# 45 small matmuls with an unread result, between the first modulation and the first projection of a hybrid backbone step

## The chip, the cores and the metric

The kernel runs as one program on one core of a Trainium2 chip. The metric is the device time of one execution in microseconds (us). Below, PE is TensorE (matmuls), PEld its loading of stationary operands, DVE is VectorE, ACT is ScalarE, POOL is GpSimd and SP the engine that issues most DMAs. PSUM is the memory that PE writes its results to: eight banks, each 512 fp32 columns on 128 partitions.

## The reference

One inference step of four layers over 128 context tokens and 512 latent tokens, 1024 features wide. Each layer modulates its input with a shift, a scale and a gate that come from a conditioning vector, runs a token mixer (differential attention, bidirectional retention, short convolution, differential attention), and ends in a residual layer norm:

```python
def ada_modulation(cvec, w_mod, b_mod):
    m = jax.nn.silu(cvec) @ w_mod + b_mod
    shift, scale, gate = jnp.split(m[:, None, :], 3, axis=-1)
    return shift, scale, gate
...
    for i in range(DEPTH):
        sh_p, sc_p, g_p = ada_modulation(c_ctx[None], w_mod[i], b_mod[i])
        sh_s, sc_s, g_s = ada_modulation(c, w_mod[i], b_mod[i])
        hp = xp * (1 + sc_p) + sh_p
        hs = xs * (1 + sc_s) + sh_s
...
            q, k, v, z = diff_project(hp, w_in_a[j])
...
        xp = layer_norm(ALPHA * xp + g_p * out_p, ln_g[i], ln_b[i])
        xs = layer_norm(ALPHA * xs + g_s * out_s, ln_g[i], ln_b[i])
```

## The kernel before

All tokens lie transposed in SBUF (`xT`: features on partitions, 640 token columns). Matrix products are made in three matmuls of rounded halves (`mm3`: high by high, low by high, high by low), so each weight block `raw` that a DMA brings in is first split into `wh` on ACT and `wl` on DVE (`convert`), and each modulated input into `hH` and `hL`.

The order of the work on the engines is fixed when the program is built: a planner walks over streams of small items with a cost for each operation, takes the item that it thinks starts soonest, and writes its instructions down. Every engine then runs its own list in order and waits on counters of the other engines (semaphores, one per engine: a wait is for a count). Which waits an instruction needs is worked out when it is written down, from the tiles and the ranges of them that it and earlier instructions read and write. All of PSUM is one tile, `ps`.

The first stage matters here. The shift and scale of layer 0 are computed in four parts of 256 features. For each part `pair_mm` does 32 plain fp32 matmuls, in two blocks of 16: the conditioning vector, padded to 32 columns (`cpad`), is the stationary operand, 128 columns of `w_mod` are the moving one, and the four results of one step `k` go to the four strips of 32 partitions of bank `m0`. `pair_vectors` then copies the 128 x 128 result to SBUF on ACT (`mdt`), transposes it on PE into columns 128 to 256 of the same bank (`tr`, line 477), adds the bias on DVE in two instructions (`mod`) and makes the scale and shift vectors `Av` and `Bv` on DVE. With them `first_h` computes the modulated input, hH on ACT and its unrounded copy `FA` on ACT or DVE; `first_lo` makes hL. The first projection of layer 0, matmuls of hH or hL with wh or wl (line 469), follows on PE. The first item that PE has after the transposition of part 0 is this projection.

A plain fp32 matmul (both operands fp32 and not rounded) is one row in the program's order and two MATMUL records in the trace, one behind the other; a transposition is one record.

Of the kernel before, what the change touches and what calls it, by code (L numbers as in the profile page):

```python
# [234 lines left out]
def kernel(ctx: ExitStack, tc: tile.TileContext, io: dict):  # L235
    nc = tc.nc
# [3 lines left out]
    def sb(name, shape, dt=F32):  # L240
        return big.tile(shape, dt, name=name)
# [14 lines left out]
    ident = sb("ident", [128, 128])  # L256
    rope0, KD, rope3 = [big.tile([128, 2 * TS], dt, name=n, tag="rope") for n, dt in (("rope0", F32), ("KD", F32R), ("rope3", F32))]
    cpad = sb("cpad", [128, KC, 32])
# [82 lines left out]
    def bank(key):  # L341
        b, n = S.held[key]
        return PS[:, b] if n == 1 else PS[:, b:b + n]

    def done(key):
        b, n = S.held.pop(key)
        S.free += range(b, b + n)
# [11 lines left out]
    def isap(x):  # L359
        return x is not None and not isinstance(x, (int, float))  # L360

    def do(eng, dur, outs, ins, emit, port=False):
        if S.rec is None:
            emit()
        else:
            S.rec.append((eng, dur, outs, [a for a in ins if isap(a)], port))
# [5 lines left out]
    def n_of(ap):  # L372
        n = 1
        for _, c in list(ap.ap)[1:]:
            n *= c
        return n

    def act(out, in_, func=ACTF.Copy, **k):
        extra = [k.get("scale"), k.get("bias")]
        outs = [out] + ([k["accum_out"]] if "accum_out" in k else [])  # L380
        d = n_of(out) / 1.2 + (51 if in_.tensor.name == PS.tensor.name else 94) + 93 * (sum(map(isap, extra)) + len(outs) - 1)
        do("ACT", d, outs, [in_] + extra, lambda: nc.scalar.activation(out=out, in_=in_, func=func, **k))  # L382

    def vtt(out, a, b, op):
        do("DVE", n_of(out) / 0.96 + 70, [out], [a, b], lambda: nc.vector.tensor_tensor(out=out, in0=a, in1=b, op=op), both(a, b))  # L385
# [23 lines left out]
    def vts(out, a, s1, s2=None, op0=ALU.mult, op1=None):  # L409
        k = {} if s2 is None else {"op1": op1}  # L410
        do("DVE", n_of(out) / 1.4 + 70 + 50 * (isap(s1) + isap(s2)), [out], [a, s1, s2],
           lambda: nc.vector.tensor_scalar(out=out, in0=a, scalar1=s1, scalar2=s2, op0=op0, **k), both(a, out))  # L412
# [13 lines left out]
    def vcopy(out, a):  # L426
        do("DVE", n_of(out) / 0.96 + 70, [out], [a], lambda: nc.vector.tensor_copy(out=out, in_=a))
# [33 lines left out]
    def mm(out, lhsT, rhs, start, stop):  # L461
        n = list(rhs.ap)[-1][1] if len(list(rhs.ap)) == 2 else n_of(rhs)
        m = n_of(lhsT)
        if lhsT.dtype == F32:
            d = n * {1: 112.0, 256: 1.88, 384: 2.5}.get(n, 1.69) if m > 32 else n / 2.4
        else:
            d = max(n / 2.4 + 13.5, 110.0 if m > 32 else 0.0)
        do("PE", d, [out], [lhsT, rhs],
           lambda: nc.tensor.matmul(out, lhsT=lhsT, rhs=rhs, start=start, stop=stop, skip_group_check=True))  # L469
# [6 lines left out]
    def tr(out, a):  # L476
        do("PE", 116.0, [out], [a], lambda: nc.tensor.transpose(out, a, ident))  # L477
# [984 lines left out]
    def pair_mm(p, ks):  # L1462
        MD = bank("m0") if ks[0] else pj("m0")
        for k in ks:
            for j in range(4):
                mm(MD[32 * j:32 * j + 32, 0:128], cpad[:, k, :], wt0[p % 2][k // 4][:, k % 4, 128 * j:128 * j + 128], k == 0, k == 7)

    def pair_vectors(p):
        MD = bank("m0")
        mt = mdt[:, 128 * (p % 2):128 * (p % 2) + 128]  # L1470
        act(mt, MD[:, 0:128])
        tr(MD[:, 128:256], mt)
        for g in range(2):
            c = slice(8 * g + 2 * p, 8 * g + 2 * p + 2)
            vtt(
                mods[0][:, c, :],
                MD[:, 128 + 64 * g:192 + 64 * g].rearrange("p (j r) -> p j r", r=32)[:, :, 0:2],
                bmod[:, 0, c].unsqueeze(2).to_broadcast([128, 2, 2]),
                ALU.add,
            )  # L1480
        done("m0")
        c = slice(2 * p, 2 * p + 2)
        vts(Av[0][:, c, :], mods[0][:, 8 + 2 * p:10 + 2 * p, :], 1.0, op0=ALU.add)
        vcopy(Bv[0][:, c, :], mods[0][:, c, :])
# [31 lines left out]
    for p in range(4):  # L1516
        if p:
            ld0.append(Item(lambda p=p: load_pair(p), need=[("m0", p - 2) if p > 1 else ("start",)], give=[("ld", p)]))
        for k in range(0, 8, 4):
            st0.append(Item(lambda p=p, k=k: pair_mm(p, range(k, k + 4)), need=[("ld", p)] if p else (),  # L1520
                            give=[("m0", p)] if k else ()))
        st0.append(Item(lambda p=p: pair_vectors(p)))
        for m in (2 * p, 2 * p + 1):
            for hf in range(2):
                need = [("lnh", -1, hf, m - 4)] if m > 3 else []
                st0.append(Item(lambda m=m, hf=hf: first_h(m, hf), need=need, give=[("t", -1, hf, m)]))
                lo0.append(Item(lambda m=m, hf=hf: first_lo(m, hf), need=[("t", -1, hf, m)], give=[("lnh", -1, hf, m)]))
            x0.append(Item(lambda m=m: first_x(m), need=[("t", -1, 1, m)], give=[("lnx", -1, 0), ("lnx", -1, 1)] if m == 7 else ()))
# [353 lines left out]
```

## Time and profile before

| | |
|---|---|
| time, median of three runs | 1816.77 us (1816.58 to 1816.88) |
| the profiled execution | 1815.59 us, of which span 1813.8 us |
| mean granted clock of PE over the span | 0.986 of full speed |
| PE busy | 1756.9 us, 97% of the span |
| PEld, DVE, ACT, POOL busy | 1652.1, 1123.9, 724.0, 128.8 us |
| DMA | 186.80 MB, mean 103 GB/s |

The span goes from the first to the last instruction on the profiled core; 1.79 us of the profiled execution lie around it. Busy shares are averages over stages with different limits, so the first 24 us are read by themselves below. The clock column (PEclk) gives the share of full speed that was granted to PE: 1.00 is 2.4 GHz, 0.50 is 1.2 GHz, a value between is a stretch with both.

### The profile page before, as it was taken

The page shows a single profiled execution, that of the slowest core. Times are in us where ns is not written, and L with a number is a line of the kernel's source. Part 1 is how long each engine was busy: PE and PEld are TensorE (multiplying, and loading weights), DVE is VectorE, ACT ScalarE, POOL GpSimd, SP SyncE. Part 2 cuts the span into 40 slices and gives each one's busy share as a digit, 9 for nine tenths or more (in the row PEclk, how much of TensorE's full clock was granted, in tenths as well). Part 3 has the DMA queues.
Part 4 walks back from the last instruction along what each step waited for, and adds up shares of the span by engine and source line. Part 5 has one row for each costly group of instructions (what it writes and reads, how often), then busy time and mean ns, then how long its engine had stood idle before and what let it go on. Part 6 is the DMA issues. An engine that isn't in the chain of part 4 may idle for free.

```text
span 1813.8 us, 31795 instructions
## 1 busy us (share of the span) xinstructions
PE 1756.9 (97%) x12756; PEld 1652.1 (91%) x12756; DVE 1123.9 (62%) x2673; ACT 724.0 (40%) x1546; POOL 128.8 (7%) x133
## 2 busy tenths in 40 slices
PE   7999999999999999999999989999999999999996
PEld 6999999999889889888888889999999999999995
DVE  3877777888726335245434674344368767778877
ACT  4555555544424323223223333222225545555441
POOL 1001000002300000000000013000003210000101
PEclk8999999999999999999999999999999999999998
DMA  9533333226312233321321351233345222222201
GB/s 348 165 114 114 114 114 96 74 73 166 107 70 97 82 115 117 105 93 57 117 93 47 116 161 50 100 129 122 105 124 150 68 67 80 81 75 63 73 16 59
DMA packets 76309, 186.80 MB, mean 103 GB/s; under 512 B 9600, under 2 KB 20992, under 8 KB 75136
## 3 DMA queue, kind: packets, MB, share of 16 engines
q1 hardware_dynamic: 74432, 178.47, 29.8%
q0 software_dynamic: 1728, 6.29, 1.9%
q8 instruction: 100, 1.64, 0.4%
q14 instruction: 49, 0.40, 0.1%
HBM read 159.04 MB, written 8.91 MB: 93 GB/s over the span
## 4 chain that ended last, share of the span: by engine, by line
PE 83%; DVE 10%; ACT 4%; issue 2%; DMA 1%; SPq 0%; POOL 0%; ACTq 0%; DVEq 0%; POOLq 0%
PE ps L469 80%; PE ps L477 4%; DVE xT L416 1%; DVE sm L416 1%; DVE wl L385 1%; ACT wh L382 1%; ACT FA L382 1%; ACT F L382 1%; DVE F L385 1%; DVE FA L439 1%; DVE xT L385 1%; DVE F L416 0%; DVE sm L430 0%; DVE FA L412 0%; DVE sm L385 0%
## 5 line engine op out<-in xcount | busy, mean ns | idle before, releaser
L469 PE MATMUL ps<-hH,wh 128*128 128x256 f32 (+1 forms) x1184 | 374.5, 316 | 4.7 <-ACT wh L382 3.1
L469 PE MATMUL ps<-hH,wl 128*128 128x256 f32 (+1 forms) x1184 | 366.6, 310 | 1.4 <-DVE wl L385 1.4
L469 PE MATMUL ps<-hL,wh 128*128 128x256 f32 (+1 forms) x1184 | 366.6, 310 | 0.0
L385 DVE TENSOR_TENSOR wl<-raw,wh 128x1024 fp32r<-128x1024 f32 (+2 forms) x177 | 208.1, 1178 | 246.4 <-ACT wh L382 245.5
L469 PE MATMUL ps<-wh,hH 128*128 128x256 f32 (+1 forms) x960 | 310.9, 324 | 1.2 <-DVE F L416 1.0
L382 ACT ACTIVATE wh<-raw 128x1024 fp32r<-128x1024 f32 (+2 forms) x198 | 198.1, 1003 | 285.1 <-PE ps L469 208.4
L469 PE MATMUL ps<-wl,hH 128*128 128x256 f32 (+1 forms) x960 | 305.9, 319 | 0.0
L469 PE MATMUL ps<-wh,hL 128*128 128x256 f32 (+1 forms) x960 | 305.8, 319 | 0.0
L469 PEld LDWEIGHTS ps<-hH,wh 128*128 128x128 f32 x1184 | 225.1, 190 | 11.1 <-issue 4.3
L469 PEld LDWEIGHTS ps<-hH,wl 128*128 128x128 f32 x1184 | 225.2, 190 | 2.1 <-DVE wl L385 1.9
L469 PEld LDWEIGHTS ps<-hL,wh 128*128 128x128 f32 x1184 | 224.9, 190 | 0.3 <-DVE hL L385 0.3
L469 PE MATMUL ps<-yh,wh 128*128 128x384 f32 (+1 forms) x640 | 203.5, 318 | 5.0 <-ACT yh L382 4.3
L469 PE MATMUL ps<-yl,wh 128*128 128x384 f32 (+1 forms) x640 | 199.4, 312 | 0.0
L469 PEld LDWEIGHTS ps<-wh,hH 128*128 128x128 f32 x960 | 182.8, 190 | 17.9 <-ACT FA L382 1.8
L469 PE MATMUL ps<-yh,wl 128*128 128x384 f32 (+1 forms) x640 | 198.9, 311 | 0.0
L469 PEld LDWEIGHTS ps<-wl,hH 128*128 128x128 f32 x960 | 182.7, 190 | 12.7
L469 PEld LDWEIGHTS ps<-wh,hL 128*128 128x128 f32 x960 | 182.8, 190 | 11.8
L382 ACT ACTIVATE FA<-FA,sm 128x640 f32<-128x640 f32 x144 | 112.0, 778 | 164.7 <-DVE sm L439 164.7
L416 DVE SCALAR_TENSOR_TENSOR xT<-ps,mod,xT 128x128 f32<-128x128 f32 (+2 forms) x312 | 121.6, 435 | 77.6 <-PE ps L469 77.3
L382 ACT ACTIVATE F<-ps 128x128 f32<-128x128 f32 (+2 forms) x336 | 97.5, 318 | 154.3 <-PE ps L469 151.7
L469 PE MATMUL ps<-RA 128*128 128x320 f32 (+2 forms) x696 | 129.5, 320 | 1.8 <-DVE F L416 1.1
L469 PEld LDWEIGHTS ps<-yh,wh 128*128 128x128 f32 x640 | 122.5, 191 | 8.5 <-ACT yh L382 4.7
(155 smaller groups left out, 2583.2 us busy)
## 6 DMA issues: line engine op xcount, KB each, us to landing
mraw<-in_w_mod SPq DMA_DIRECT2D x160, 256.0 KB, 4.6
raw<-in_wqk_a SPq DMA_DIRECT2D x32, 512.0 KB, 3.5
raw<-in_wvz_a SPq DMA_DIRECT2D x32, 512.0 KB, 4.0
raw<-in_wvg_b SPq DMA_DIRECT2D x32, 512.0 KB, 3.3
raw<-in_win_c SPq DMA_DIRECT2D x32, 512.0 KB, 3.2
RA<-RA SPq DMA_DIRECT2D x32, 320.0 KB, 4.0
raw<-in_wqk_b SPq DMA_DIRECT2D x16, 512.0 KB, 3.2
raw<-in_wout_b SPq DMA_DIRECT2D x16, 512.0 KB, 3.2
```

Source lines behind the costliest of these rows:

```text
L382: do("ACT", d, outs, [in_] + extra, lambda: nc.scalar.activation(out=out, in_=in_, func=func, **k))
L385: do("DVE", n_of(out) / 0.96 + 70, [out], [a, b], lambda: nc.vector.tensor_tensor(out=out, in0=a, in1=b, op=op), both(a, b))
L416: lambda: nc.vector.scalar_tensor_tensor(out=out, in0=a, scalar=s, in1=b, op0=op0, op1=op1), both(a, b))
L439: do("DVE", n_of(out) / 0.96 + 68, [out, mx], [a], lambda: nc.vector.tensor_tensor_reduce(out=out, in0=a, in1=z, scale=-0.125, scalar=3.0e ...
L469: lambda: nc.tensor.matmul(out, lhsT=lhsT, rhs=rhs, start=start, stop=stop, skip_group_check=True))
L477: do("PE", 116.0, [out], [a], lambda: nc.tensor.transpose(out, a, ident))
```

## The change

`stay_awake` writes fp32 matmuls of one `cpad` block with the identity matrix, 32 output partitions by 128 columns, into columns 256 to 384 of bank `m0`, partitions 0 to 31, which nothing reads. For part 0 alone, five of them stand ahead of the transposition and forty behind it.

```diff
+    def stay_awake(MD, n):
+
+        for i in range(n):
+            do("PE", 0.0, [MD[0:32, 256:384]], [cpad[:, i % 8], ident],
+               lambda i=i: nc.tensor.matmul(MD[0:32, 256:384], lhsT=cpad[:, i % 8, :], rhs=ident, start=True, stop=True, skip_group_check=True))
+
     def pair_vectors(p):
         MD = bank("m0")
         mt = mdt[:, 128 * (p % 2):128 * (p % 2) + 128]
         act(mt, MD[:, 0:128])
+        if p == 0:
+            stay_awake(MD, 5)
         tr(MD[:, 128:256], mt)
+        if p == 0:
+            stay_awake(MD, 40)
         for g in range(2):
             c = slice(8 * g + 2 * p, 8 * g + 2 * p + 2)
             vtt(
```

The planner counts them as 0 ns, so that the rest of every engine's list stands as before. On PE, from the second block of part 0 (the `cpad` rows) to the first projection (`ps<-hH,wh`), with the engines whose counters a row waits for in brackets (DMAHW are DMA queues):

```order
 L469 MATMUL ps<-F_92,cpad 32x128 [waits DMAHW2_49]
 L469 MATMUL ps<-F_92,cpad 32x128 x15
-L477 MATMUL ps<-ident,mdt 128x128 [waits DMAHW3_49,Activation_49]
+L1472 MATMUL ps<-ident,cpad 32x128 [waits DMAHW3_49,Activation_49]
+L1472 MATMUL ps<-ident,cpad 32x128 x4
+L477 MATMUL ps<-ident,mdt 128x128
+L1472 MATMUL ps<-ident,cpad 32x128 x40
 L469 MATMUL ps<-hH,wh_73 128x256 [waits Activation_49]
 L469 MATMUL ps<-hH,wl_77 128x256 [waits DVE_49]
```

The 45 new rows stand around the transposition, and the wait for ACT (the copy of the bank to `mdt`) that the transposition had now stands at the first of them. On DVE, from the padding of `cpad` to the vectors `Av` and `Bv`; the first `mod` row is the bias add of part 0:

```order
 L412 TENSOR_SCALAR cvec<-cvec 128x16 [waits DVE_49]
 L427 COPY cpad<-cvec 128x8x2 [waits DVE_49]
-L385 TENSOR_TENSOR mod_107<-ps,bmod 128x4 [waits DMAHW4_49,PE_49]
+L385 TENSOR_TENSOR mod_107<-ps,bmod 128x4 [waits DMAHW4_49,PE_49,Activation_49]
 L385 TENSOR_TENSOR mod_107<-ps,bmod 128x4
 L412 TENSOR_SCALAR Av_109<-mod_107 128x4 [waits DVE_49]
```

The bias add waits for PE in both; only its wait for ACT is new in these rows. The count of PE that it waits for is not printed in them; in the built programs it is 33 before (16 and 16 for the two blocks of `pair_mm`, 1 for the transposition) and 78 now, and PE now adds its 46 (45 new matmuls and the transposition) in one step, at the last of the forty.

## Rows read from the trace of the kernel before

**Rows 1.** The page: busy time by engine, and the granted clock in 40 slices.
```profile
PE 1756.9 (97%) x12756; PEld 1652.1 (91%) x12756; DVE 1123.9 (62%) x2673; ACT 724.0 (40%) x1546; POOL 128.8 (7%) x133
...
PEclk8999999999999999999999999999999999999998
```

**Rows 2.** The chain that ended last, 9 to 22 us: start, us, what.
```profile
9.10 1.55 PE ps L469 x32
...
10.67 0.29 ACT mdt L382
10.96 0.04 issue
11.00 0.34 PE ps L477
11.34 0.02 issue
11.37 0.24 DVE mod L385 x2
...
11.91 0.49 ACT hH L382
...
18.05 1.24 DVE wl L385
19.28 0.04 issue
19.32 2.86 PE ps L469 x26
```

**Rows 3.** Stretches of the first 40 us: busy us by engine, PEclk, DMA share, GB/s.
```profile
11.40:13.40 2.00, 0.00 (x0) 0.00 (x0) 0.79 (x5) 1.49 (x4) 0.15 (x1) 1.00 1.03 418
13.40:14.10 0.70, 0.00 (x0) 0.00 (x0) 0.00 (x0) 0.70 (x2) 0.58 (x1) 0.51 1.04 421
14.10:19.30 5.20, 3.29 (x7) 1.86 (x7) 4.33 (x7) 4.86 (x9) 1.53 (x2) 0.50 1.00 415
19.30:23.60 4.30, 4.28 (x40) 3.57 (x41) 1.57 (x2) 0.00 (x0) 0.00 (x0) 0.50 1.07 414
23.60:24.30 0.70, 0.70 (x6) 0.45 (x5) 0.00 (x0) 0.00 (x0) 0.00 (x0) 0.96 0.99 398
24.30:40.00 15.70, 15.70 (x193) 14.64 (x196) 8.42 (x24) 9.14 (x20) 2.91 (x3) 1.00 1.03 399
```

**Rows 4.** PE in order of time: start, busy us, instruction, idle before.
```profile
11.00 0.33 PE L477 MATMUL ps<-ident,mdt 128*128 128x128 f32 x1 [0.41 <-ACT mdt L382]
...
14.17 0.58 PE L469 MATMUL ps<-hH,wh 128*128 128x256 f32 x1 [2.84 <-ACT wh L382]
...
20.69 1.94 PE L469 MATMUL ps<-F,cpad 128*32 128x128 f32 x32
...
24.29 1.08 PE L469 MATMUL ps<-FA,cpad 128*32 128x128 f32 x32
```

**Rows 5.** PE in order of time at full clock: projection, plain fp32, transpositions.
```profile
111.82 0.28 PE L469 MATMUL ps<-wh,hL 128*128 128x256 f32 x1
111.94 0.28 PE L469 MATMUL ps<-wl,hH 128*128 128x256 f32 x1
112.06 1.06 PE L469 MATMUL ps<-F,FA 128*128 128x128 f32 x8
...
422.35 1.03 PE L477 MATMUL ps<-ident,xT 128*128 128x128 f32 x8
```

**Rows 6.** Records of PE with the tile `cpad`: ns min/median/max, first and last start.
```profile
L469 PE MATMUL ps<-F,cpad x192: 272/283/423, 6.5 to 40.7; 128*32 128x128 f32 x192
L469 PE MATMUL ps<-FA,cpad x64: 272/273/297, 24.3 to 43.4; 128*32 128x128 f32 x64
```

**Rows 7.** Later stretches of 20 us with a low clock: PE busy, PEclk, DMA share, GB/s.
```profile
800.00:820.00 20.00, 17.54 (x87) 0.83 0.15 53
1020.00:1040.00 20.00, 16.37 (x109) 0.83 0.64 179
1060.00:1080.00 20.00, 17.53 (x160) 0.91 0.67 204
1080.00:1100.00 20.00, 18.25 (x134) 0.91 0.25 81
1480.00:1500.00 20.00, 19.33 (x143) 0.91 0.19 61
```

## The prediction

> **What bounds the kernel now.** The page comes first: PE is busy for 97% of the span, and its clock is granted in full nearly everywhere except in the first slice, the last one and a few between [rows 1]. So time lost or won on PE counts in full, unless PE is waiting for somebody where it is won. The change sits in the first 24 us, so I read that stage alone. The chain of waits [rows 2] shows it without a gap: the second block of modulation matmuls (from 9.10), ACT's copy to mdt (10.67), the transposition (11.00), the bias add on DVE (11.37), Av and Bv, then ACT without a pause from 11.91 and DVE's split of wl at 18.05, until PE takes over at 19.32. The reader is to see that the bias add at 11.37 is a link of the chain: nothing runs beside it that could absorb a delay, since ACT's next work (hH at 11.91) needs its result, and each engine runs its list in order.
>
> The stretches [rows 3] show what the filler is placed against. PE does nothing from 11.4 to 13.4 and ACT and DVE set the pace. The clock is still 2.4 GHz until 13.4, is at 1.2 GHz when the first projection begins at 14.17 [rows 4], stays there while PE works in pieces and for 4.3 us in which it works without a pause (19.30 to 23.60), and is up again at 23.66: the 0.96 between 23.60 and 24.30 means 0.06 us at half speed. From there PE is busy all the time (15.70 of 15.70) at full clock.
>
> **The low clock is the most that the change can win.** Until 19.3 PE waits for ACT and DVE, so that a faster PE would only wait longer. From 19.32 to 23.66 it is the bound, at half speed: 4.34 us of which half, 2.2 us, could be saved. That is 0.12% of the time, less than the 0.2% (3.6 us) that a measurement of this kernel tells from no change.
>
> **What the filler costs, price first.** No row shows a filler matmul, so its price is bounded by the nearest rows. A plain fp32 matmul is two records. With four strips abreast, 32 records (16 matmuls) took 1.08 us from 24.29 on [rows 4], the last of them 0.27 [rows 6]: eight turns of four, seven steps in 0.81 us, 0.116 us a turn, or 0.0675 us a matmul over the whole row. In one strip nothing is abreast, and a record follows a record: eight records of full-width fp32 matmuls took 1.06 us [rows 5], less a last one of 0.27 that is 0.79 for seven steps, 0.112 us; eight transpositions give (1.03 - 0.27) / 7 = 0.108. All 45 fillers write to partitions 0 to 31, which is one strip, so I take a turn for each of the 90 records, 0.108 to 0.116, and 0.110 as the value: 0.22 us a matmul. The low end of the price is the 0.0675 of the row with four strips. The high end is the same turn at the low clock: the row at 20.69 [rows 4], 32 records in 1.94 us with a last one of 0.42 [rows 6], gives (1.94 - 0.42) / 7 = 0.217.
>
> The Trainium skill speaks to this price ("TensorE: Matmul & The Clock Gate", Part 3: Packing small matmuls): small matmuls run at the same time when their outputs lie in different strips of 32 partitions. By that rule the 45, all in one strip, run one after the other; the rows with four strips abreast agree with it (0.0675 against 0.22 us a matmul), and no row shows one narrow strip alone.
>
> **What waits for the filler.** The five ahead of the transposition wait for ACT's copy as it did, so they start at 11.00 and move it by 10 x 0.110 = 1.1 us. The forty behind it take 80 x 0.110 = 8.8 us. They would lie in PE's idle time up to 14.17 if the bias add waited for the transposition alone. It doesn't: the count that the built program has it wait for is reached at the last of the forty. So the add comes after all 45: 90 x 0.110 = 9.9 us later (9.7 to 10.4 with 0.108 and 0.116). The last filler record is about as long as the transposition's (0.27 against 0.33), so the step from its start to the add stays near the 0.37 us of before; -0.05 I leave out.
>
> The Trainium skill has the rule behind this wait ("PSUM — Partial Sum Buffer", PSUM bank collisions raise a hardware error): PSUM is to be guarded by the bank and not by the address. By it a filler in bank m0 holds up a reader of other columns of m0; the built program's count agrees, and a filler in another bank would not be in the way. By the address alone the cost would be that of the last rival below.
>
> **What is queued behind the add.** On DVE: Av, Bv, FA, the split of wl. On ACT: hH, FA and the conversion of the first weights, all behind the wait for Bv. On PE, the whole first projection. POOL waits for hH. On SP the loads into buffers that those steps free. DMAs already issued go on, and are done early, but the chain holds no DMA from 9.10 on [rows 2] and PE is busy without a pause from 24.3 to 40 [rows 3], so an earlier landing gives nothing. All of 11.37 to 19.32 moves as a block, and PE's bound stretch behind it. Cover: none, since the gap that the filler was to fill opens only behind the add. **Sum of this term: +9.9 us.**
>
> **The clock behind the filler.** After the last filler PE is idle for the same 2.84 us as before (the chain from the add to 14.17 is unchanged), and then works in the same pieces. In before that sequence ended in the low clock, so I let it do so again: 0. Bounds: the clock is up for the projection after all, -2.2; or the fall and rise lie otherwise against the work, up to +1. Five later low stretches [rows 7], each following a lull of PE, cost between 0.09 x 20 x 2 = 3.6 and 0.17 x 20 x 2 = 6.8 us at half speed each; moved by 10 us, one of them may come out longer or shorter, so I allow 2 us to either side, and 0 as the value.
>
> **Result.** Profiled execution: 1813.8 + 9.9 = 1823.7 span, with 1.79 around it 1825.5. The median of the runs lies 1.18 above the profiled execution, so the forecast is 1816.77 + 9.9 = 1826.7 us, 0.54% slower; its own range is 1823.5 to 1829.5.
>
> **The rivals.**
> - *The clock falls during the filler.* Only one strip in four of the array works, and in before the clock fell at 13.4. From 11.00 to 13.4 then fit (2.4 - 0.11) / 0.110 = 21 records, the other 69 take 0.217 each, 15.0 us, and the add comes at about 28.7, 17.3 us late: 1834.1. For it: no row has one strip alone. Against it: PE is busy without a pause from 11.00 on, and every fall in the rows follows a lull.
> - *The clock stays up through the first projection.* Then 9.9 - 2.2 = 7.7: 1824.5. Against it: the lull behind the filler. The Trainium skill ("TensorE: Matmul & The Clock Gate", Why this matters for your kernels) asks for no long idle gaps between bursts of matmuls, which is what a filler is for; by that rule the clock would stay up only if the filler stood in the gap, and the rows 3 agree that it falls in the gap.
> - *The filler is cheap (not slower).* If matmuls into one strip flow at the rate of the rows with four, 0.0675 us, then the add is 45 x 0.0675 = 3.0 us late: 1819.8, no change that can be told. It decides below 3.6 / 45 = 0.08 us a matmul. Against it: the turns of full-width records, 0.112 each and two to a matmul.
> - *The add doesn't wait for the forty.* Then it is 1.1 us late, the forty end at 12.2 + 8.8 = 21.0, the twelve projection matmuls that PE does from 14.17 to 20.69 run behind them at full clock (0.12 us from one to the next [rows 5]) until 22.4, and what took from 20.69 to 23.66 at half speed takes 1.5: 23.9 against 23.66, +0.2, 1817.0. Against it: the count of 78.
>
> **How the numbers follow.** Chances: forecast 0.72, clock falls in the filler 0.13, clock stays up 0.06, cheap filler 0.05, no wait for the forty 0.04. The first three are slower by over 0.2%, 0.91; the last two are within 0.2%, less 0.02 that I leave for a low stretch that drops out and makes it faster: 0.07 and 0.02. The range has to leave out no more than 2 in 10: the forecast's own range holds some 0.70 of all, with the clock that stays up (1824.5, inside it) 0.76, and only with the slow filler 0.89. So it runs from 1823.5 to 1834.5.
>
> **What the profile after would show.** Right: 90 records of ps<-ident,cpad in about 9.9 us from 11.0, DVE's first mod add released by PE at about 21.2 and no longer by the transposition, ACT's hH at 21.8, the first projection at 24.1 with a lull of some 2.8 us before it, at the low clock; PE in continuous work from 29.2. Wrong: a mod add near 12.5 (the wait), records closer than 0.1 us (the price), a clock under 1.00 before 21 us (the fall), or 1.00 from 24 to 34 us (the clock that stays up).

## The result, and the profile after

The changed kernel takes 1826.84 us (median of four, 1825.76 to 1827.36) against 1816.67 us before (1815.92 to 1816.88): ratio 1.0059, 95% interval 1.0045 to 1.0073, slower by some 10 us. 1826.7 was forecast. The profiled execution is the longest of the four, 1827.36 us with a span of 1825.6. One execution, 3474.76 us in the run with the five alone below, was slow for a reason that no trace shows, and the ratio of that run leaves it out.

The first stage of the changed kernel in order of time (start, busy us, engine, line, instruction, idle before and its releaser), which answers to [rows 2, 4]:

```profile
9.12 1.94 PE L469 MATMUL ps<-F,cpad 128*32 128x128 f32 x32 [0.78 <-DMA F<-in_w_mod]
11.12 0.28 ACT L382 ACTIVATE mdt<-ps 128x128 f32<-128x128 f32 x1 [8.35 <-PE ps L469]
11.45 2.34 PE L1472 MATMUL ps<-ident,cpad 128*32 128x128 f32 x10 [0.40 <-ACT mdt L382]
13.73 0.48 PE L477 MATMUL ps<-ident,mdt 128*128 128x128 f32 x1
14.13 9.33 PE L1472 MATMUL ps<-ident,cpad 128*32 128x128 f32 x80
23.56 0.23 DVE L385 TENSOR_TENSOR mod<-ps,bmod 128x4 f32<-128x4 f32 x2 [20.15 <-PE ps L1472]
...
24.10 0.49 ACT L382 ACTIVATE hH<-xT,Bv,Av 128x128 fp32r<-128x128 f32 x1 [12.70 <-DVE Bv L427]
...
26.36 0.38 PE L469 MATMUL ps<-hH,wh 128*128 128x256 f32 x1 [2.90 <-ACT wh L382]
...
31.52 0.58 PE L469 MATMUL ps<-hH,wl 128*128 128x256 f32 x1 [0.68 <-DVE wl L385]
...
36.34 1.08 PE L469 MATMUL ps<-FA,cpad 128*32 128x128 f32 x32
```

The reader is to see three things. The transposition (L477) starts at 13.73, but the first bias add (mod) starts at 23.56, 0.10 us after the last of the 80 records behind it, and its releaser is now L1472, the filler. The first projection starts at 26.36, 2.80 us after the add; before it was 14.17 and 11.37, also 2.80. And the lull of PE ahead of the projection is there again, 2.90 us against 2.84: the filler does not lie in it.

Stretches of the changed kernel (length, busy us and records of PE, PEld, DVE, ACT, POOL, PEclk, DMA share, GB/s), for [rows 3]:

```profile
13.70:15.10 1.40, 1.40 (x7) 1.01 (x7) 0.00 (x0) 0.00 (x0) 0.00 (x0) 1.00 1.04 433
15.10:23.50 8.40, 8.37 (x77) 8.10 (x75) 0.00 (x0) 0.00 (x0) 0.00 (x0) 1.00 1.04 414
23.50:26.40 2.90, 0.04 (x1) 0.04 (x1) 0.88 (x6) 2.30 (x5) 0.73 (x1) 1.00 0.99 393
26.40:28.70 2.30, 0.85 (x3) 0.44 (x3) 2.30 (x4) 2.30 (x6) 0.81 (x1) 0.99 0.76 242
28.70:35.50 6.80, 5.90 (x43) 4.35 (x44) 3.55 (x5) 2.46 (x3) 0.73 (x1) 0.50 0.20 73
35.50:50.00 14.50, 14.50 (x178) 13.31 (x178) 6.42 (x20) 7.18 (x16) 2.20 (x2) 1.00 0.90 320
```

DVE, ACT and POOL do nothing at all from 13.7 to 23.5. The clock falls to 1.2 GHz near 28.7, in the pieces of the first projection, and PE works its way out of the low clock by 35.5, as it did by 23.66 before. From 15.10 on the filler makes a record each 0.109 us; ahead of that the records take twice as long (7 in 1.40 us), although the column reads 1.00. Ahead of the first change of the clock that the trace holds, the column is thus no guide; the lengths of the records show that it was the low clock.

### The profile page after: what moved, and what is told of

The parts are those of the page before. It is cut to its first block, busy times and chain, and to the rows that moved or that the text cites. A ratio compares the mean times of both kernels' runs of the same rounds, so it can differ in the third digit from the quotient of the medians.

```text
span 1825.6 us, 31975 instructions
## 1 busy us (share of the span) xinstructions
PE 1767.6 (97%) x12846; PEld 1661.9 (91%) x12846; DVE 1123.5 (62%) x2673; ACT 724.0 (40%) x1546; POOL 129.3 (7%) x133
## 4 chain that ended last, share of the span: by engine, by line
PE 83%; DVE 10%; ACT 4%; DMA 2%; issue 2%; SPq 0%; POOL 0%; ACTq 0%; DVEq 0%; POOLq 0%
PE ps L469 79%; PE ps L477 3%; DVE xT L416 1%; DVE sm L416 1%; DVE wl L385 1%; ACT wh L382 1%; ACT FA L382 1%; DVE xT L385 1%; ACT F L382 1%; DVE F L385 1%; DVE FA L439 1%; DMA F<-in_w_mod 1%; DVE FA L412 1%; DVE F L416 0%; DVE RA L385 0%
## 5 line engine op out<-in xcount | busy, mean ns | idle before, releaser
L469 PEld LDWEIGHTS ps<-wh,hL 128*128 128x128 f32 x960 | 182.9, 191 | 11.8
```

## The experiments

All ratios are to the kernel before, run on the same chip; intervals are 95%.

**The same work into another bank.** The fillers write to bank 7, and in the trace of this kernel no instruction waits for one of them.

```diff
-            stay_awake(MD, 5)
+            stay_awake(PS[:, 7], 5)
...
-            stay_awake(MD, 40)
+            stay_awake(PS[:, 7], 40)
```

> The same 45 matmuls at the same places of PE's list, but they write to a bank that nothing uses at that time, so that no count of theirs is waited for. Theory (the wait): the cost of the change is that the bias add comes behind all 45. Then the add comes 0.7 to 1.5 us later than in the kernel before (the five, which may now start during ACT's copy), the forty run beside DVE's and ACT's work until 21 to 23 us, and the time is 0 to 2 us above the kernel before (ratio 1.000 to 1.001). Rival (the work itself): 45 matmuls on the engine that is busy for 97% of the span cost their own 9.9 to 11.7 us wherever their result goes: ratio 1.0054 to 1.0064, as with the change.

Measured: 1816.92 us, ratio 1.0004 (0.9995 to 1.0013). Its first stage in order of time:

```profile
11.01 1.63 PE L1472 MATMUL ps<-ident,cpad 128*32 128x128 f32 x10
11.31 0.28 ACT L382 ACTIVATE mdt<-ps 128x128 f32<-128x128 f32 x1 [8.75 <-PE ps L469]
12.58 0.33 PE L477 MATMUL ps<-ident,mdt 128*128 128x128 f32 x1
12.84 8.92 PE L1472 MATMUL ps<-ident,cpad 128*32 128x128 f32 x80
12.94 0.23 DVE L385 TENSOR_TENSOR mod<-ps,bmod 128x4 f32<-128x4 f32 x2 [9.76 <-PE ps L477]
```

PE does the same 90 records, and the add starts beside them, released by the transposition. The add is 1.57 us later than in before: the five stand ahead of it, and the second block (1.93 us) and part of the five (1.63) ran at the low clock here. The stretches of the same kernel show why 10 us of work cost next to nothing:

```profile
11.00:21.70 10.70, 10.70 (x100) 10.06 (x91) 5.97 (x12) 7.33 (x13) 2.26 (x3) 1.00 1.03 409
21.70:23.30 1.60, 1.60 (x13) 1.48 (x12) 0.75 (x2) 0.00 (x0) 0.00 (x0) 1.00 1.01 419
23.30:40.00 16.70, 16.70 (x218) 15.31 (x218) 7.18 (x21) 7.93 (x18) 2.68 (x3) 1.00 1.03 400
```

While PE is in the filler, ACT (7.33 us) and DVE (5.97) get the projection's operands ready, and PE then takes its first twelve matmuls in 1.6 us at 2.4 GHz. Two things nearly cancel: the filler keeps PE until 21.7, some 2.4 us beyond the 19.32 from which it worked without a pause before, and what it did at half speed until 23.66 it now does at full speed. The work is not the cost; the wait is.

**Only the last filler in the bank of the add.**

```diff
-            stay_awake(MD, 40)
+            stay_awake(PS[:, 7], 39)
+            stay_awake(MD, 1)
```

(The five are in bank 7 too.)

> As the run with the other bank (45 matmuls in it, ratio 1.0004), but the very last of the forty writes to the bank of the bias add again. Theory (what costs is the wait for the last filler, and only the bank of its result decides on it): the add comes behind the last filler again, at 21 to 23 us, and the time is that of the change less what the five hide under ACT's copy: 9 to 10 us above before, ratio 1.0050 to 1.0058. Rival (writing to the bank itself is slow or collides, so that the cost is shared out over the fillers): one matmul in 45 costs next to nothing, ratio 1.0005.

Measured: 1826.20 us, ratio 1.0052 (1.0040 to 1.0064). In order of time:

```profile
12.28 8.92 PE L1472 MATMUL ps<-ident,cpad 128*32 128x128 f32 x80
21.30 0.23 DVE L385 TENSOR_TENSOR mod<-ps,bmod 128x4 f32<-128x4 f32 x2 [17.91 <-PE ps L1472]
```

One matmul of 45 is moved back, and the loss is back: ratio 1.0052 against 1.0004 with all of them in bank 7. Writing to the bank of the add is not slow: at full clock the records are 0.109 us apart there (77 in 8.37 us in the changed kernel, from 15.10 on) and 0.1095 in bank 7 ((8.92 - 0.27) / 79 in the run above). The count that the add waits for is the cost.

**Four strips instead of one.**

```diff
-            do("PE", 0.0, [MD[0:32, 256:384]], [cpad[:, i % 8], ident],
-               lambda i=i: nc.tensor.matmul(MD[0:32, 256:384], lhsT=cpad[:, i % 8, :], rhs=ident, start=True, stop=True, skip_group_check=True))
+            o = MD[32 * (i % 4):32 * (i % 4) + 32, 256:384]
+            do("PE", 0.0, [o], [cpad[:, i % 8], ident],
+               lambda i=i, o=o: nc.tensor.matmul(o, lhsT=cpad[:, i % 8, :], rhs=ident, start=True, stop=True, skip_group_check=True))
```

> The 45 matmuls stay in the bank of the bias add, with its wait, but go in turn to its four strips of 32 partitions. Theory (the price is a turn of 0.11 us for each record of one strip, and four strips share a turn): 45 matmuls take 3.0 us at full clock (0.0675 each) and 5.5 at half, the add comes that much later and the time is 3 to 5.5 us above before (ratio 1.0017 to 1.0030). Rival (a small matmul has its price whatever strip it goes to): 0.22 us each, 9.9 us or more, ratio 1.0054 or more as with the change.

Measured: 1820.24 us, ratio 1.0024 (1.0013 to 1.0034). In order of time:

```profile
11.49 1.06 PE L1473 MATMUL ps<-ident,cpad 128*32 128x128 f32 x10 [0.40 <-ACT mdt L382]
...
12.89 4.24 PE L1473 MATMUL ps<-ident,cpad 128*32 128x128 f32 x80
17.27 0.23 DVE L385 TENSOR_TENSOR mod<-ps,bmod 128x4 f32<-128x4 f32 x2 [14.08 <-PE ps L1473]
```

The forty take 4.24 us, 0.106 a matmul, which lies between the full and the low clock of the rows with four strips (1.08 / 16 = 0.0675 and 1.94 / 16 = 0.121 [rows 4]), and is still under half of the 8.92 that one strip takes at full clock. The wait is whole; the price is the turn of a strip.

**Eighty behind the transposition.**

```diff
-            stay_awake(MD, 40)
+            stay_awake(MD, 80)
```

> Eighty instead of forty behind the transposition, nothing else. Theory (the add waits for the last of them, 0.22 us each at full clock): forty more cost 40 x 0.22 = 8.8 us more, 18.7 to 21 us above before (ratio 1.0103 to 1.0116), and the add comes at about 32 us. Rival (the price rises or falls with their number, since the clock falls while one strip in four works): 40 x 0.43 = 17 us more, 27 us above before, with a granted clock of 0.50 in the filler; or, where part of them is hidden, under 5 us more.

Measured: 1836.30 us, ratio 1.0115 (1.0100 to 1.0131), 9.5 us above the change in the medians (10.2 by the ratios) for 40 more matmuls of 0.22 us, 8.8. Two timeline rows and a stretch (PE, PEld, DVE, ACT, POOL, PEclk) of it:

```profile
14.17 17.65 PE L1472 MATMUL ps<-ident,cpad 128*32 128x128 f32 x160
31.92 0.23 DVE L385 TENSOR_TENSOR mod<-ps,bmod 128x4 f32<-128x4 f32 x2 [28.66 <-PE ps L1472]
...
14.20:31.80 17.60, 17.60 (x161) 17.35 (x160) 0.00 (x0) 0.00 (x0) 0.00 (x0) 1.00 0.80 314
```

The add comes behind the last filler again, at 31.92. 160 records in 17.65 us, the last of 0.27, are 0.1093 apart, and the column shows 1.00: with one strip of four kept busy for 17.6 us the clock did not fall.

**The five alone.**

```diff
-        if p == 0:
-            stay_awake(MD, 40)
```

> The five ahead of the transposition alone, in the bank of the bias add as in the change; no forty. Theory (all 45 stand ahead of the add, each with its price): the add comes 1.1 us later at full clock and 2.1 to 2.3 at half, ratio 1.0006 to 1.0013; the forty then make the other 8 to 9 us of the change. Rival (the wait for ACT's copy or the switch between narrow and full matmuls is what costs, once, whatever their number): near the whole 10 us, ratio 1.005.

Measured: 1817.90 us, ratio 1.0003 (0.9995 to 1.0012). The trace has the step that was expected: ten records from 11.29, the transposition at 12.51, the add at 12.93. In the time it can't be told from nothing; the ratio lies below the expected 1.0006 to 1.0013, and its interval holds nearly all of that and no room for 10 us. So the forty make the loss.

**Twelve, in the lull alone.**

```diff
-        if p == 0:
-            stay_awake(MD, 5)
...
-            stay_awake(MD, 40)
+            stay_awake(PS[:, 7], 12)
```

> None ahead of the transposition, twelve behind it into a bank that nothing uses at that time: 12 x 0.22 = 2.6 us in the 2.84 us in which PE is idle ahead of the first projection. Theory (the wait is the whole cost): the add comes at the time of before, 11.4 us, and the time is not above before. If the filler in the gap also holds the clock up until the projection works without a pause, up to 2.2 us below before (ratio 0.9988); if the clock falls in the pieces behind the gap all the same, as I expect, the ratio is 1.000 within 0.0007. Rival (the work itself costs): 2.6 us above, ratio 1.0014.

Measured: 1815.21 us, ratio 0.9992 (0.9983 to 1.0001): not above before, and a gain not proven. The add is released by the transposition (11.95, with the transposition at 11.44; later than the 11.37 of before, since the second block took 1.93 us), and the clock came down later than in [rows 3]: the first matmul of the projection lasts 0.39 us at 14.97, where the low clock made it 0.58, and one at 20.51, behind another without a pause, lasts 0.41, where full clock makes it 0.28. So a filler in the lull alone is not enough to hold it, as expected.

**Fillers in every wait of the first stage.** Twelve behind the transposition, and 4, 3, 2, 2 and 4 behind five of the first seven projection matmuls, all into bank 5.

```diff
...
+                    for j, (a, b) in enumerate(((wh, H), (wl, H), (wh, L))):
+                        mm(ps, a[:, k], b, k == 0 and j == 0, False)
+                        stay_awake(PS[:, 5], pieces[3 * k + j])
...
-            stay_awake(MD, 40)
+            stay_awake(PS[:, 5], 12)
```

(`pieces` holds the five numbers, and zeros for the other matmuls; no filler stands ahead of the transposition.)

> No filler ahead of the transposition; twelve behind it and 4, 3, 2, 2 and 4 behind the first matmuls of the first projection, where PE waits for ACT and DVE, all 27 into a bank that is not in use. If nothing waits for them and they hold the clock up until the projection works without a pause, the stretch that ran at half speed (4.3 us) takes half: about 2 us below before, ratio 0.9988 to 0.9992. Rival (the pieces come late at times and delay the projection by what they save): ratio 1.000. Second rival (a filler costs its own PE time): 5.9 us above, ratio 1.003.

Measured: 1815.25 us, ratio 0.9989 (0.9981 to 0.9997), faster than before by 0.11%, with an interval that ends just short of 1. Its stretches:

```profile
11.00:16.50 5.50, 5.10 (x31) 3.92 (x25) 2.40 (x8) 4.10 (x9) 1.06 (x2) 1.00 1.02 418
16.50:23.00 6.50, 6.50 (x44) 4.68 (x42) 4.32 (x6) 3.23 (x5) 1.21 (x2) 1.00 1.03 402
23.00:40.00 17.00, 17.00 (x221) 15.57 (x220) 7.42 (x21) 8.19 (x19) 2.93 (x3) 1.00 1.03 401
```

Once up, the clock does not fall again in the first 40 us. The twelve began at the low clock in this execution and took 4.63 us, more than the lull; at 1818.05 us it is the slowest of its twelve executions, so that the gain is seen in the median and not in this trace.

**The same, and awake from the start.** Eight more ahead of the first modulation block, while PE waits for its weights, and one ahead of the second.

```diff
+        if p == 0:
+            wake(1 if ks[0] else 8)
         for k in ks:
             for j in range(4):
```

(`wake` is `stay_awake` with columns of `cpad` in place of the identity matrix, into bank 5.)

> As the run before with 27 fillers in the waits of PE, and eight more ahead of the first block of modulation matmuls, while PE waits for its weights, and one ahead of the second block. If the clock is then up for the second block, that block takes 1.1 us and not 1.9 on the chain: 0.8 us less than the run with 27, ratio to before 0.9980 to 0.9988. Rival (the first block waits for the fillers, 9 x 0.43 us at half speed from 3.3 us on): ratio as with the 27 or 0.5 us above it.

Measured: 1814.33 us, ratio 0.9987 (0.9978 to 0.9995). In order of time:

```profile
9.22 1.08 PE L469 MATMUL ps<-F,cpad 128*32 128x128 f32 x32
10.36 0.28 ACT L382 ACTIVATE mdt<-ps 128x128 f32<-128x128 f32 x1 [7.57 <-PE ps L469]
10.70 0.33 PE L477 MATMUL ps<-ident,mdt 128*128 128x128 f32 x1 [0.40 <-ACT mdt L382]
10.95 2.81 PE L1491 MATMUL ps<-ident,cpad 128*32 128x128 f32 x24
11.06 0.23 DVE L385 TENSOR_TENSOR mod<-ps,bmod 128x4 f32<-128x4 f32 x2 [7.64 <-PE ps L477]
...
13.92 0.38 PE L469 MATMUL ps<-hH,wh 128*128 128x256 f32 x1 [0.16 <-ACT wh L382]
...
22.64 1.08 PE L469 MATMUL ps<-FA,cpad 128*32 128x128 f32 x32
```

The second block takes 1.08 us where it took 1.94 in the run before this one, the twelve now fit the lull (2.81 us, 0.16 of idle time left), and the block with FA starts at 22.64; in [rows 4] it started at 24.29. This version beats both kernels: before by the ratio above, and the change by 12.5 us in the medians. That the early fillers add to the 27 is seen in the trace and not in the times, whose intervals overlap.

## Why the prediction was right, point by point

- **Which wait.** It said that the add comes behind all 45, since the count that it waits for is reached at the last one. Shown: by the releaser in the profile, by bank 7 (ratio 1.0004), and by one matmul put back (1.0052).
- **The price.** 0.110 us a record was taken; 80 records in 8.92 us, less the last of 0.27, are 0.1095 apart, and 160 are 0.1093. The rival with a cheap filler fell; four strips show where its price belongs.
- **The size.** 9.9 us was the sum, 10.2 the difference of the medians. The interval of the ratio allows 8.2 to 13.3 us, so an agreement to 0.3 is partly luck. In the profiled executions the add is 12.19 us later and the span 11.8 longer (1825.6 against 1813.8). Of what the add has beyond the sum, 0.44 is there because the second modulation block ran at the low clock throughout (1.94 us; 1.50 in before, and no filler is ahead of it), and the other 1.8 because the five, the transposition and the first few of the forty did too (2.34 us for ten records, where 1.1 was taken). That term was not in the sum: the text took the clock of before, which rose within the second block, for granted. It named a clock under 1.00 ahead of 21 us as a sign against it; there was a low clock until 15.1, but as a late rise and not as a fall. In the run with one filler put back, where the clock rose earlier, the ten took 1.31 us.
- **No cover.** The chain from the add to the projection kept its 2.80 us, and the lull came back behind the filler.
- **The clock behind the filler.** It fell, but not where the text had it, in the lull: it fell in the pieces of the projection, whose first matmul ran at full clock (0.38 us at 26.36, 0.58 in before), and the low stretch then lasted until 35.5. That saved next to nothing of the rival's 2.2 us, since PE waits for ACT and DVE there: from the add to PE's work without a pause are 7.96 us (23.56 to 31.52), and 7.95 before (11.37 to 19.32). The block with FA comes 12.05 us later, 0.14 less than the add. Where the fall lies differs between executions: in the lull in before and with eighty (0.58 us for the first matmul of the projection), behind it here, with the five alone and with one filler put back (0.38). The rival with a clock that falls during the filler is out: 17.6 us in one strip at 1.00.
- **The later low stretches.** One got shorter: in before 800 to 820 us showed 0.83, some 6.8 us at half speed [rows 7]; in the changed kernel 820 to 840 shows 0.91, 3.6 us. Half of the difference would be 1.6 us, but it gave back only some 0.5, within the 2 us allowed. ACT's same two instructions ahead of and behind the stretch, in before and in the changed kernel:

```profile
806.26 1.06 ACT L382 ACTIVATE wh<-raw 128x1024 fp32r<-128x1024 f32 x1 [5.97 <-PE ps L469]
815.17 0.69 ACT L382 ACTIVATE FA<-ps,dec 128x512 f32<-128x512 f32 x1 [2.24 <-PE ps L469]
...
818.47 1.06 ACT L382 ACTIVATE wh<-raw 128x1024 fp32r<-128x1024 f32 x1 [5.97 <-PE ps L469]
826.86 0.69 ACT L382 ACTIVATE FA<-ps,dec 128x512 f32<-128x512 f32 x1 [2.43 <-PE ps L469]
```

The first comes 12.21 us later, the second 11.69. The 10 us of the filler are not what decides it: from 800 to 820 us the run with the five alone shows 0.91 too, and the one with all 45 in bank 7 shows 0.83.

## What to carry to other kernels

A filler is free only if nobody waits for it: look up the count that the next reader of its bank waits for, and give it a bank of its own. It must also lie in the wait, which here was split into a lull of 2.8 us and, at full clock, five short ones (0.26 to 0.87 us in the run with twelve). Filling all of them paid 0.11%. Filling the lull alone made 0.08%, which is not clear of nothing, and the two are not told apart. A filler with a reader behind it cost 0.59%. An engine that is busy for 97% of a span can still take 10 us of extra work for next to nothing in the one stage where it waits for others.

## What the runs showed that was not expected

PE's clock rose for the first time at different moments of the same stage in different executions. The second modulation block, the same instructions ahead of any filler, took 1.50 us in the profile of before, 1.78 in the run with the five alone, and 1.93 or 1.94 in seven others. The kernel before ranged from 1813.5 to 1818.4 us over 29 runs on one chip and from 1814.1 to 1819.1 over 23 on another, wider than the 0.3 us of the first three. How much of that range the moment of the first rise explains was not measured. A single profile of so short a stage thus carries an offset of 0.4 us ahead of any filler, and of up to 1 us more in the ten records of the five (1.28, 2.11 and 2.34 us in three kernels that are alike up to there), that has nothing to do with the change.
